# Two transformer layers in one kernel: layer 0's down projection as seven block products, with a new product order and modulation sums moved

## The chip, the cores and the metric

The kernel is one program on one core of a Trainium2 chip. The metric is device time in microseconds (us) for the whole program. All work is done by five engines with queues of their own: PE (TensorE, matrix products), DVE (VectorE), ACT (ScalarE), POOL (GpSimd) and SP (SyncE, which here issues most of the transfers). They meet through semaphores.

## The reference

Two layers on 1024 latent tokens of width 1024, beside 256 context tokens. Layer 0 mixes tokens with a gated MLP (gMLP), layer 1 with windowed attention; each is followed by a convolutional gated feed-forward network (ConvGLU). Cut to what matters here:

```python
def conv_ffn(h, w_up, conv_w, conv_b, w_down):
    a, b = jnp.split(h @ w_up, 2, axis=-1)
    ap = jnp.pad(a, ((0, 0), (1, 1), (0, 0)))
    a = ap[:, :-2] * conv_w[0] + ap[:, 1:-1] * conv_w[1] + ap[:, 2:] * conv_w[2] + conv_b
    return (jax.nn.gelu(a) * b) @ w_down
...
for i in range(DEPTH):
    mod_lat = (silu_c @ ada_w[i] + ada_b[i])[:, None, :]
    mod_ctx = (silu_cc @ ada_w[i] + ada_b[i])[None, None, :]
    sh1, sc1, g1, sh2, sc2, g2 = jnp.split(mod_lat, 6, axis=-1)
    ...
    x = x + g1 * rms_norm(y, norm_g[i, 1])
    h = modulate(rms_norm(x, norm_g[i, 2]), sh2, sc2)
    x = x + g2 * rms_norm(conv_ffn(h, ...), norm_g[i, 3])
```

The feed-forward width is 2816, or 22 blocks of 128. The same network also runs on the context tokens in layer 0; in layer 1 only the latent tokens are needed.

## The kernel before

Every fp32 product is made as three matmuls of 128x512 on parts of fewer bits: an operand x is split into xh (ACT's copy to a shorter format) and xl (DVE's x - xh), and hi*hi, hi*lo and lo*hi are summed in PSUM. So each weight or activation that comes in costs one ACT and one DVE operation before PE can use it. In names, wh/wl are the parts of weights, ah/al those of activations, "raw" (three buffers) is where most loads land, "row" a general tile of 128x1024 (ten buffers). PSUM is used as two psA tiles of two banks each and four psB tiles of one bank.

The stages on the time axis are: gMLP in two passes (`gmlp`: five token tiles, then five more, line 773), layer 0's feed-forward (`lat_ffn`, line 941, called on line 1651: its up stage on context, then on the latent tokens, then its down stage, then `ctx_down` for the context), attention, and layer 1's feed-forward (called on line 2058).

**Up stage.** For each block f of the 22 it makes seven products out of eight (sums of blocks of activations against sums of blocks of weights, a Winograd-Strassen scheme), then convolves, gates, and stores the result `actd[f]` in memory. ACT, DVE and POOL make the sums of weights, DVE the sums of results. The last f also runs `lead_in`, which loads the first operands of the down stage early.

**Layer 0's down stage** (in `lat_ffn`, `for h in range(2)`) is a plain loop: for each half h of the 1024 output columns, over 22 blocks n, over eight token tiles i, three matmuls into bank i: four banks of psA, four of psB. A half's banks are drained by `finish`, in the order of the tiles, then the other half begins on the same banks.

**Layer 1's down stage** (`down_blocks`, line 1338) uses seven products. The token tiles are split into two halves (i and i + 4), the columns into two of 512, and the 22 blocks into 11 pairs (f0, f1). Products p1 and p2 and p4 read activations as they are; p3, p5, p6 and p7 read the four sums of a pair. `pair_sums` makes those during the up stage: it loads both `actd` blocks, DVE adds four times, and stores the sums in `actc`. Eleven pairs are walked as six groups of two (the last has one). A product is 11 x 4 banks x 3 = 132 matmuls; p2 is added on top of p1 in the A banks (psA), the others use B banks (psB). `after(p)` drains banks to SBUF when a product ends: p1 by ACT's copies (s1), the others by DVE's adds into `ys`, which collects the result y. The weights' sums are made by DVE when a group is fetched (`fetch`, three groups ahead). The order was: p1, p6, p2's first group, p7, p2's second, p4, p2's third, p5, p3, and p2's last three groups as the tail, bank by bank, so that each token tile can leave as soon as its bank is done.

**Modulation sums.** mod_lat and mod_ctx are vectors of 6 x 1024 per layer, each piece called (l, m). A piece is summed by DVE over eight loads of 512 KB of `ada_w` (one operation of 128x1024 per load and per stream: latent, context), then turned into columns by PE's transposes (`ada_cols`). `ada_steps(l, m, streams)` is such a generator, and `step(gen)` runs it one step on at chosen points of a stage. Layer 0's pieces 0 to 4 are made in the gMLP passes. Layer 1's pieces 0, 1 (both streams), 3 and 4 (latent) are summed during layer 0's down stage (`sums_of`) and transposed during `ctx_down`.

The order in which each engine finally works is set by a scheduler from this program order and the buffers; the waits come from tiles: an operation that writes a PSUM tile waits for earlier readers of that tile, also when they read another bank of it.

Of the kernel before, what the change touches and what calls it, by code (L numbers as in the profile page):

```python
# [15 lines left out]
P = 128  # L16
D = 1024
# [15 lines left out]
def hybrid_kernel(  # L33
# [739 lines left out]
    def gmlp(si, hb, tiles, gate, extra, between, pre_last, on_flip=None, head=None, order=(0, 1, 2, 3, 4), mod=None):  # L773
# [5 lines left out]
        for nb in range(4):  # L779
# [3 lines left out]
            for u in range(4 if nb or not head else 0):  # L783
# [13 lines left out]
                if nb > 0:  # L797
                    step(extra)
# [142 lines left out]
    def lat_ffn(l, stage, n0, halos, gate, between, steady, ctx=None, after=None):  # L941
# [98 lines left out]
        def pair_sums(n, f0, f1):  # L1040
# [9 lines left out]
            V.tensor_tensor(out=s2, in0=s1, in1=a11, op=ALU.subtract)  # L1050
            Q.dma_start(actc[0:2, n].rearrange("s p c -> p s c"), u.rearrange("p (s c) -> p s c", s=2))
            yield
            V.tensor_tensor(out=s3, in0=a11, in1=a21, op=ALU.subtract)
            yield
            V.tensor_tensor(out=s4, in0=a12, in1=s2, op=ALU.subtract)
            Q.dma_start(actc[2:4, n].rearrange("s p c -> p s c"), w.rearrange("p (s c) -> p s c", s=2))
# [176 lines left out]
        for (f, how), nxt in zip(jobs, jobs[1:] + [None]):  # L1233
# [6 lines left out]
            if ctx is None:  # L1240
                fill_up[0] = sums_
# [7 lines left out]
        if ctx is None:  # L1249
# [3 lines left out]
        open_pool("down%d" % l)  # L1253
        pool = stage_pool["pool"]
        ks = list(range(n0, NF)) + list(range(n0))
        ys, sums = {}, []
        KEEP = 5
        if ctx is not None:
            extra = chain(*[sums_of(pool, sums, 1, m, streams)
                            for m, streams in ((0, (0, 1)), (1, (0, 1)), (3, (0,)), (4, (0,)))])  # L1260
        else:
            extra = iter(())

        def act_hl(k, own):
            raw = t_raw()
            Q.dma_start(raw, actd[k, :, 0:SEQ])
            hl = [t_w("w" + z) if own else pool.tile([P, 1024], F32R, name=nm("a" + z), tag="a" + z, bufs=7 if ctx is None else 6)
                  for z in "hl"]
            split_into(hl, raw)
            return hl  # L1270

        def finish(t, h, p, part):
            hs = slice(h * 512, (h + 1) * 512)
            junk = pool.tile([P, 512], mybir.dt.bfloat16, name=nm("junk"), tag="junk", bufs=2)
            if h == 0:
                ys[t] = pool.tile([P, 1024], F32, name=nm("y"), tag="y%d" % t, bufs=1)
            return gated(p, gate(t)[:, hs], ys[t][:, hs], part, junk)

        parts, hls = {}, {}
        for h in range(2):  # L1280
            pair = [psA() for _ in range(2)]
            banks = [pair[i // 2][:, i % 2, :] for i in range(4)] + [psB() for _ in range(4)]
            ws = {}

            def step_(n, i):
                (ah, al), (wh, wl) = hls[ks[n]], ws[n]
                tk = slice(i * P, (i + 1) * P)
                mm3(banks[i], ah[:, tk], al[:, tk], wh, wl, n == 0, n == NF - 1)

            def fetch(n):  # L1290
                if h == 0 or n >= KEEP:
                    hls[ks[n]] = act_hl(ks[n], h == 0 and n < 2)
                if n % 2 == 0:
                    raw = t_raw()
                    for j in range(2):
                        Q.dma_start(raw[:, j * 512:(j + 1) * 512],
                                    w_down[l][ks[n + j] * P:(ks[n + j] + 1) * P, h * 512:(h + 1) * 512])
                    hi, lo = t_w("wh"), t_w("wl")
                    split_into((hi, lo), raw)
                    for j in range(2):  # L1300
                        ws[n + j] = hi[:, j * 512:(j + 1) * 512], lo[:, j * 512:(j + 1) * 512]

            nk = NF - (2, 6 if ctx is None else 5)[h]
            if h == 1:
                ks.reverse()
            for n in range(nk):
                fetch(n)
                for i in range(8):
                    step_(n, i)
                if h or n < 14:  # L1310
                    step(extra, 1 + (n % 4 == 1))
            for n in range(nk, NF):
                fetch(n)
            for i in range(8):
                for n in range(nk, NF):
# [786 lines left out]
```

## Time and profile before

| what | value |
|---|---|
| time, median of 3 runs | 2903.92 us (2899.92 to 2905.09) |
| the profiled execution | 2896.91 us |
| its span | 2895.1 us |
| mean granted PE clock | 0.988 |
| PE busy | 2765.4 us, 14702 instructions |
| DVE busy | 2112.9 us, 3175 instructions |
| ACT busy | 1371.5 us |
| POOL busy | 676.2 us |
| DMA | 513.78 MB, mean 177 GB/s |

Times of windows and timelines are us from the start of the span. All operations go through one wrapper, so every row of the profile carries the same line (L50), and tiles tell them apart: `psA<-wh,ah` is a matmul of weights' high part and activations' high part into a psA tile. Stages begin at about: gMLP 66 and 400, layer 0's up stage 771 (context) and 917 (latent), its down stage 1343 and 1585 (context), attention 1655, layer 1's up stage 2240, its down stage 2670.

### The profile page before, as it was taken

What the parts mean: (1) busy time and instruction counts of PE and PEld (TensorE: products, weight loads), DVE (VectorE), ACT (ScalarE), POOL (GpSimd) and SP (SyncE); (2) the same over time, 40 slices, a digit from 0 to 9 for tenths busy, and PEclk for the clock granted to TensorE, in tenths of its full rate; (3) what the DMA queues carried; (4) which work ended last, traced back from release to release, by engine and by line L of the source; (5) the groups of instructions that cost most, each with busy time, mean ns of one, the idle gap of its engine ahead of it and who ended that gap; (6) DMA issues with size and microseconds to landing.
All of it is one profiled execution on the core that took longest, in us unless ns stands there. A gap on an engine that the chain in (4) does not pass through costs nothing. (4 is left out here: it accounts for less than half of the span.)

```text
span 2895.1 us, 40248 instructions
## 1 busy us (share of the span) xinstructions
PE 2765.4 (96%) x14702; PEld 2379.7 (82%) x14702; DVE 2112.9 (73%) x3175; ACT 1371.5 (47%) x2298; POOL 676.2 (23%) x1002
## 2 busy tenths in 40 slices
PE   7999999999999999999999999899996999999999
PEld 5798988899898888888877777788885988888787
DVE  6557675755887888778743669887876688888766
ACT  4332342322575444544323534777875444445333
POOL 1150130620201122220003024565552112111001
PEclk9999999999999999999999999999998999999999
DMA  8764357522585333546855865346576345445754
GB/s 260 242 192 151 112 175 220 169 89 83 187 236 178 111 100 117 167 160 210 299 167 174 281 209 193 114 156 234 173 238 200 107 152 188 150 152 178 244 180 149
DMA packets 418200, 513.78 MB, mean 177 GB/s; under 512 B 18641, under 2 KB 298065, under 8 KB 418001
## 3 DMA queue, kind: packets, MB, share of 16 engines
q1 hardware_dynamic: 361585, 448.01, 48.3%
q10 hardware_dynamic: 55264, 58.99, 6.0%
q0 software_dynamic: 1152, 4.19, 0.4%
q8 instruction: 116, 1.90, 0.3%
q14 instruction: 83, 0.68, 0.1%
HBM read 403.12 MB, written 108.00 MB: 177 GB/s over the span
## 5 line engine op out<-in xcount | busy, mean ns | idle before, releaser
L50 PE MATMUL psB<-cmb,wh 128*128 128x512 f32 (+2 forms) x2584 | 748.4, 374 | 5.8 <-ACT row L50 2.3
L50 ACT CAST wh<-raw 128x1024 fp32r<-128x1024 f32 (+1 forms) x378 | 334.1, 897 | 484.2 <-PE psB L50 178.6
L50 PEld LDWEIGHTS psB<-cmb,wh 128*128 128x128 f32 x2584 | 471.5, 188 | 95.5 <-ACT row L50 3.4
L50 PE MATMUL psB<-cmb,wl 128*128 128x512 f32 (+2 forms) x1292 | 482.6, 374 | 0.0
L50 DVE TENSOR_TENSOR wl<-raw,wh 128x1024 fp32r<-128x1024 f32 (+1 forms) x378 | 386.1, 1033 | 110.8 <-ACT wh L50 109.4
L50 PE MATMUL psB<-wh,big 128*128 128x512 f32 x864 | 286.3, 399 | 2.6 <-ACT big L50 1.3
L50 PEld LDWEIGHTS psB<-cmb,wl 128*128 128x128 f32 x1292 | 243.1, 188 | 43.5
L50 POOL TENSOR_SCALAR sm<-sm 128x1 f32<-128x1 f32 (+1 forms) x76 | 43.4, 572 | 925.9 <-ACT junk L50 371.8
L50 POOL TENSOR_TENSOR row<-raw,raw 128x512 f32<-128x512 f32 x44 | 73.7, 1675 | 594.2 <-DMA raw<-in_f_w_up_dram 477.1
L50 ACT CAST wh<-row 128x512 fp32r<-128x512 f32 (+1 forms) x152 | 120.2, 793 | 183.7 <-DVE row L50 95.0
L50 PE MATMUL psB<-wh,act 128*128 128x512 f32 x640 | 199.9, 390 | 1.6 <-DVE tmp L50 1.6
L50 PEld LDWEIGHTS psB<-wh,big 128*128 128x128 f32 x864 | 164.0, 191 | 39.5 <-ACT big L50 2.4
L50 PE MATMUL psA<-big,wh 128*128 128x320 f32 x1024 | 193.4, 311 | 2.8 <-ACT wh L50 1.7
L50 DVE SCALAR_TENSOR_TENSOR row<-row,cwcols,row 128x1024 f32<-128x1024 f32 (+2 forms) x142 | 153.2, 1079 | 36.6 <-ACT row L50 20.6
L50 ACT CAST ah<-raw 128x1024 fp32r<-128x1024 f32 (+1 forms) x77 | 77.5, 1010 | 192.3 <-PE psB L50 111.9
L50 PE MATMUL psB<-wl,big 128*128 128x512 f32 x432 | 167.0, 396 | 0.0
L50 PEld LDWEIGHTS psA<-big,wh 128*128 128x128 f32 x1024 | 159.8, 188 | 3.8 <-ACT wh L50 2.2
L50 DVE TENSOR_TENSOR al<-raw,ah 128x1024 fp32r<-128x1024 f32 (+1 forms) x77 | 90.2, 1174 | 94.0 <-ACT ah L50 93.9
L50 PE MATMUL psB<-wh,ah 128*128 128x512 f32 x388 | 152.0, 393 | 3.9 <-ACT wh L50 3.9
L50 POOL TENSOR_SCALAR row<-row,sm,sm 128x128 f32<-128x128 f32 x160 | 121.0, 771 | 147.6 <-DMA row<-vscr 133.3
L50 PE MATMUL psB<-wl,ah 128*128 128x512 f32 x388 | 152.2, 392 | 0.0
L50 PE MATMUL psB<-wh,al 128*128 128x512 f32 x388 | 152.0, 392 | 0.0
(277 smaller groups left out, 6193.6 us busy)
## 6 DMA issues: line engine op xcount, KB each, us to landing
raw<-in_f_w_up_dram SPq DMA_DIRECT2D x142, 512.0 KB, 4.6
raw<-in_a_w_in_dram SPq DMA_DIRECT2D x64, 512.0 KB, 4.7
raw<-in_ada_w_dram SPq DMA_DIRECT2D x64, 512.0 KB, 4.8
wh<-woscr SPq DMA_DIRECT2D x48, 512.0 KB, 4.8
raw<-actd SPq DMA_DIRECT2D x44, 512.0 KB, 4.7
actd<-row SPq DMA_DIRECT2D x39, 512.0 KB, 2.6
raw<-in_a_w_out_dram SPq DMA_DIRECT2D x35, 512.0 KB, 3.5
xT<-row ACTq DMA_DIRECT2D x33, 512.0 KB, 5.0
```

The costliest lines, as they stand in the source:

```text
L50: ins = fn(*a, **kw)
```

## The change

1. Layer 0's down projection now goes through `down_blocks` too, with a flag `inner`; the plain loop is gone. Layer 0's up stage therefore runs `pair_sums` and `lead_in`. `pair_sums` works in place, on two row tiles instead of four.
2. The products come in the order p1, p2, p6, p7, p4, p5, p3, in both layers; the last three groups of p3 are the tail. p5 and p3 have their banks C in psA. Each bank is drained right after its own last matmul. Loads of the weights that several products share come later.
3. A finished token tile goes to `leave`, which in layer 0 starts `lat_tail` (norm, store, flip into the next stage); the flips of tiles 4 to 7 wait for `held`.
4. Layer 1's modulation pieces 3 and 4 go to gMLP pass 0, pieces 0 and 1 (both streams) to pass 1, with more frequent steps.

The diff, cut to its core:

```diff
-                if nb > 0:
-                    step(extra)
+                if nb > 0 or not head:
+                    step(extra, 1 + (u % 2 if head else 0))
...
-            step(extra, 2 - f % 2)
+            step(extra, 2 if head else 2 - f % 2)
+        step(extra, 99)
...
-            u, w = t_row(), t_row()
-            s1, s2, s3, s4 = u[:, 0:512], u[:, 512:1024], w[:, 0:512], w[:, 512:1024]
-            V.tensor_tensor(out=s1, in0=a21, in1=a22, op=ALU.add)
...
+            V.tensor_tensor(out=a22, in0=a21, in1=a22, op=ALU.add)
+            yield
+            V.tensor_tensor(out=a21, in0=a11, in1=a21, op=ALU.subtract)
+            yield
+            V.tensor_tensor(out=a11, in0=a22, in1=a11, op=ALU.subtract)
+            Q.dma_start(actc[0:2, n].rearrange("s p c -> p s c"), r0.rearrange("p (s c) -> p s c", s=2))
+            yield
+            V.tensor_tensor(out=a12, in0=a12, in1=a11, op=ALU.subtract)
+            Q.dma_start(actc[2:4, n].rearrange("s p c -> p s c"), r1.rearrange("p (s c) -> p s c", s=2))
...
-                return W, lead_in() if ctx is None else iter(())
+                return W, lead_in()
...
-            if ctx is None and n >= 2 and n % 2 == 0:
+            if n >= 2 and n % 2 == 0:
                 step(sums_, 9)
                 sums_ = pair_sums(n // 2 - 1, *pairs[n // 2 - 1])
...
-        if ctx is None:
-            step(sums_, 9)
-            down_blocks(l, stage, gate, pairs, pair_sums(len(pairs) - 1, *pairs[-1]), early)
-            return
...
+        step(sums_, 9)
+        down_blocks(l, stage, gate, pairs, pair_sums(len(pairs) - 1, *pairs[-1]), early, ctx is not None)
         if ctx is not None:
-            step(extra, 99)
-            ctx_down(l, stage, gate, chain(*[ada_cols(1, m, st, accs, True) for m, st, accs in sums]), after)
+            ctx_down(l, stage, gate, after)
...
-        kinds = {"p5": 0, "p6": 1, "p7": 2, "p3": 3}
+        kinds = {"p6": 0, "p7": 1, "p3": 2, "p5": 3}
...
-        fillers = {"p6": 0, "p7": 1, "p4": 2}
-        for p in ("p1", "p6", "p7", "p4", "p5", "p3"):
-            seq += [(p, g) for g in range(NG)]
-            if p in fillers:
-                seq.append(("p2", fillers[p]))
-        tail = [("p2", g) for g in range(3, NG)]
...
+        order = ("p1", "p2", "p6", "p7", "p4", "p5", "p3")
+        seq = [(p, g) for p in order for g in range(NG)]
+        TAIL = 3
...
+                elif p == "p5":
+                    pc = [psA() for _ in range(2)]
+                    C = [pc[i // 2][:, i % 2, :] for i in range(4)]
+            banks = A if p in ("p1", "p2") else B if p in ("p6", "p7", "p4") else C
...
+                    mms(banks[i], p, g, [j], i, fresh and j == 0, last)
+                    if last:
+                        after(p, i)
...
+            for p, g in seq[-TAIL:]:
+                mms(C[i], p, g, list(range(len(members[g]))), i, False, g == NG - 1)
+            after("p3", i)
+            ss = gated(ys[i][:, 512:1024], gate(i)[:, 512:1024], ys[i][:, 512:1024], parts[i], junk(512))
+            leave(i, ss)
...
-    gmlp(1, hold["h"], MIX, gate_of(0, 2), chain(ada_steps(0, 3, (0, 1)), ada_steps(0, 4, (0, 1))),
+    gmlp(1, hold["h"], MIX, gate_of(0, 2), chain(ada_steps(0, 3, (0, 1)), ada_steps(0, 4, (0, 1)), ada_steps(1, 0, (0, 1)), ada_steps(1, 1, (0, 1))),
```

What this moves on the engines, in the compiled order, at three places.

PE in layer 1's down stage, where p1 ends, before. psA_24938 is p1's second two-bank tile; psB_25191 to 25194 are p6's banks:

```order
12617 L50 MATMUL psA_24938<-wh_25075,ah_25071 128x512
12618 L50 MATMUL psA_24938<-wl_25076,ah_25071 128x512
12619 L50 MATMUL psA_24938<-wh_25075,al_25072 128x512
12620 L50 MATMUL psB_25191<-wh_25116,ah_25112 128x512 [waits PE_49,Activation_49]
12621 L50 MATMUL psB_25192<-wh_25116,ah_25112 128x512 [waits PE_49]
```

The same place now. psA_25079 and psA_25080 are p1's and p2's two tiles; wh_25245 is p2's first weight:

```order
12488 L50 MATMUL psA_25079<-wh_25204,ah_25200 128x512 [waits Activation_49]
12489 L50 MATMUL psA_25079<-wl_25205,ah_25200 128x512
12490 L50 MATMUL psA_25079<-wh_25204,al_25201 128x512
12491 L50 MATMUL psA_25080<-wh_25204,ah_25200 128x512 [waits Activation_49]
12492 L50 MATMUL psA_25080<-wl_25205,ah_25200 128x512
12493 L50 MATMUL psA_25080<-wh_25204,al_25201 128x512
12494 L50 MATMUL psA_25079<-wh_25245,ah_25241 128x512 [waits Activation_49]
```

Before, p6 went on in other tiles. Now p1's last matmuls into the second bank of each tile wait for ACT, which drains the first, and p2's first one waits for ACT again. The same pattern stands where p5 ends and p3 begins, with DVE as the engine that drains.

SP's queue at the start of layer 1's down stage, before. row_24980 and 24981 hold the last pair's sums, raw_25103 is p6's first operand:

```order
906 L50 DMA raw_25064<-actd 128x512 [waits DMAHW1_49,Activation_49]
907 L50 DMA actc<-row_24980 128x2x512 [waits DMAHW2_49,DVE_49]
908 L50 DMA actc<-row_24981 128x2x512 [waits DMAHW3_49,DVE_49]
909 L50 DMA r_4267_24912<-in_f_w_down_dram 128x512 [waits DMAHW4_49]
910 L50 DMA r_4271_24916<-in_f_w_down_dram 128x512 [waits DMAHW5_49]
911 L50 DMA r_4271_24916<-in_f_w_down_dram 128x512 [waits DMAHW6_49]
912 L50 DMA r_4287_24932<-in_f_w_down_dram 128x512 [waits DMAHW7_49]
913 L50 DMA r_4287_24932<-in_f_w_down_dram 128x512 [waits DMAHW0_49]
914 L50 DMA raw_25103<-actc 128x2x512 [waits DMAHW1_49,Activation_49]
```

And now, where raw_25235 and row_25238 are p2's first activations and weights, raw_25275 its second activations, and row_25190 and 25191 the last pair's sums:

```order
979 L50 DMA raw_25235<-actd 128x512 [waits DMAHW2_49,Activation_49]
980 L50 DMA raw_25235<-actd 128x512
981 L50 DMA row_25238<-in_f_w_down_dram 128x512 [waits DMAHW4_49]
982 L50 DMA row_25238<-in_f_w_down_dram 128x512 [waits DMAHW5_49]
983 L50 DMA actc<-row_25190 128x2x512 [waits DMAHW6_49,DVE_49]
984 L50 DMA actc<-row_25191 128x2x512 [waits DMAHW7_49,DVE_49]
985 L50 DMA raw_25275<-actd 128x512 [waits DMAHW0_49,Activation_49]
```

The second product's first loads stand ahead of the stores of the last sums, and they read `actd`, not `actc`.

DVE in one f of layer 0's up stage, before. row<-psB are the sums of results, cwcols the convolution, gate the modulation sums for the gate:

```order
939 L50 TENSOR_TENSOR row_9252<-row_9252,s_9270 128x2x256
940 L50 TENSOR_TENSOR row_9252<-psB_9217,row_9252 128x2x256
941 L50 TENSOR_TENSOR wl_9329<-raw_9218,wh_9328 128x512
942 L50 TENSOR_TENSOR wl_9329<-raw_9219,wh_9328 128x512
943 L50 TENSOR_TENSOR row_9306<-psB_9216,s_9238 128x2x256
```

And now, in every second f:

```order
996 L50 TENSOR_TENSOR row_9313<-row_9313,s_9331 128x2x256
997 L50 TENSOR_TENSOR row_9355<-row_9354,row_9355 128x512
998 L50 TENSOR_TENSOR row_9354<-row_9354 128x512
999 L50 TENSOR_TENSOR row_9354<-row_9355,row_9354 128x512
1000 L50 TENSOR_TENSOR row_9355<-row_9355,row_9354 128x512
1001 L50 TENSOR_TENSOR row_9313<-psB_9278,row_9313 128x2x256
1002 L50 TENSOR_TENSOR wl_9395<-raw_9279,wh_9394 128x512
```

The four adds of a pair (row_9354 and row_9355) stand together, ahead of the operation that reads the next bank of results.

More of the change, by code (lines that the diff above doesn't have):

```diff
@@ L1264, in act_hl @@
[L1264 to L1315, printed above, removed]
-                    step_(n, i)
-                if h == 0:
-                    parts[i] = finish(i, 0, banks[i], EPS)
-                    continue
-                ss = finish(i, 1, banks[i], parts[i])
-                if ctx is not None:
-                    active.append(lat_tail(stage, i, ys[i], ss))
-                    tick()
-                    continue
-                xr = t_row()
-                Q.dma_start(xr[:, 0:1024], src_row(stage, i))
-                r = t_sm(1)
-                G.tensor_tensor(out=r, in0=ss, in1=mhalf, op=ALU.pow)
-                for q in range(2):
-                    hs = slice(q * 512, (q + 1) * 512)
-                    V.scalar_tensor_tensor(out=xr[:, hs], in0=ys[i][:, hs], scalar=r, in1=xr[:, hs],
-                                           op0=ALU.mult, op1=ALU.add)
-                    Q.dma_start(out[0, i * P:(i + 1) * P, hs], xr[:, hs])
@@ L1334, in lat_ffn, with down_blocks @@
-        if ctx is not None:
-            step(extra, 99)
-            ctx_down(l, stage, gate, chain(*[ada_cols(1, m, st, accs, True) for m, st, accs in sums]), after)
-    def down_blocks(l, stage, gate, pairs, rest, early):
+        step(sums_, 9)
+        down_blocks(l, stage, gate, pairs, pair_sums(len(pairs) - 1, *pairs[-1]), early, ctx is not None)
+        if ctx is not None:
+            ctx_down(l, stage, gate, after)
+    def down_blocks(l, stage, gate, pairs, rest, early, inner):
         open_pool("down%d" % l)
@@ L1385, in fetch @@
             for second, m in side_loads.get((p, g), ()):
+                if second and m not in r22:
+                    r22[m] = t_row()
                 w_part((r12, r22)[second][m], m, second, 1)
@@ new lines, in lower @@
+        def lower(t):
+            ss = t_sm(1)
+            S.activation(junk(1024), ys[t], AF.Square, accum_out=ss)
+            G.tensor_scalar(out=ss, in0=ss, scalar1=1.0 / D, scalar2=EPS, op0=ALU.mult, op1=ALU.add)
+            V.tensor_tensor(out=ys[t], in0=ys[t], in1=gate(t), op=ALU.mult)
+            leave(t, ss)
+        parts, held, chores = {}, [True], []
+        order = ("p1", "p2", "p6", "p7", "p4", "p5", "p3")
+        seq = [(p, g) for p in order for g in range(NG)]
+        TAIL = 3
@@ L1525, in down_blocks @@
             while chores:
-                chores.pop(0)()
-            for p, g in tail:
-                mms(A[i], p, g, list(range(len(members[g]))), i, False, g == NG - 1)
-            final(i, A[i])
-    def sums_of(pool, sums, l, m, streams):
-        accs = [pool.tile([P, 1024], F32, name=nm("dacc"), tag="dacc%d%d" % (m, s), bufs=1) for s in streams]
-        yield from ada_sums(l, m, streams, accs,
-                            lambda: pool.tile([P, 1024], F32, name=nm("araw"), tag="araw", bufs=2))
-        sums.append((m, streams, accs))
@@ L1537, in lat_tail @@
-    def lat_tail(stage, t, y, ss):
+                lower(chores.pop(0))
+            for p, g in seq[-TAIL:]:
[3 more added lines that the diff above has]
+            leave(i, ss)
+            if inner:
+                tick()
+    def lat_tail(stage, t, y, ss, held, wide):
         xr = t_row()
@@ L1545, in lat_tail, with ctx_down @@
         S.dma_start(xs[stage + 1][t * P:(t + 1) * P, :], xr)
-        for _ in range(4):
+        while held[0]:
             yield 0
-        flip(stage + 1, t, y, True)
-    def ctx_down(l, stage, gate, cols, after):
+        for _ in range(4 if wide else 1):
+            yield 0
+        flip(stage + 1, t, y, wide)
+    def ctx_down(l, stage, gate, after):
         banks = [[psB() for h in range(2)] for i in range(2)]
@@ L1592, in ctx_down @@
                 pass
-            step(cols, 99)
             build_h = after()
```

134 lines of the change are left out of this document (46 added, 88 removed).

## The prediction

> **What bounds the kernel now.** I read the page first, for the shares of the engines; then the chain of waits, for what TensorE waits on; then the windows by stage, for what each stage leaves idle; and last the timelines where the chain or the windows showed a hole. The page:
>
> ```profile
> span 2895.1 us, 40248 instructions
> PE 2765.4 (96%) x14702; PEld 2379.7 (82%) x14702; DVE 2112.9 (73%) x3175; ACT 1371.5 (47%) x2298; POOL 676.2 (23%) x1002
> ```
>
> TensorE is busy 96% of the span, VectorE 73%. The time is the number of matmuls and the few holes between them. By stage (the columns are start:end, length, busy time and count of PE, PEld, DVE, ACT, POOL, then granted clock, DMA share, GB/s):
>
> ```profile
> 66.00:400.00 334.00, 328.99 (x1826) 292.59 (x1825) 219.69 (x334) 115.09 (x159) 71.58 (x102) 1.00 0.55 172
> 400.00:770.00 370.00, 366.59 (x2004) 325.26 (x2004) 227.82 (x319) 125.28 (x176) 101.57 (x119) 1.00 0.47 148
> 917.00:1338.00 421.00, 419.74 (x1851) 347.49 (x1852) 336.98 (x385) 203.85 (x299) 83.39 (x94) 1.00 0.39 128
> 1343.00:1585.00 242.00, 237.30 (x1050) 195.51 (x1048) 140.57 (x127) 77.24 (x104) 20.96 (x35) 0.99 0.66 225
> 1585.00:1655.00 70.00, 63.16 (x311) 50.70 (x309) 48.74 (x64) 38.36 (x50) 12.05 (x16) 0.98 0.88 285
> 2330.00:2670.00 340.00, 336.01 (x1660) 283.15 (x1659) 283.43 (x361) 163.86 (x256) 65.63 (x78) 1.00 0.50 164
> 2670.00:2890.00 220.00, 214.92 (x932) 176.03 (x930) 158.85 (x164) 89.78 (x111) 12.34 (x19) 0.98 0.59 193
> ```
>
> The rows are the two gMLP passes, layer 0's up stage on the latent tokens, its down stage, the context's down stage, layer 1's up stage (most of it) and layer 1's down stage. In the up stages and gMLP passes TensorE idles for 1.3 to 5.0 us of hundreds, so work added to other engines there costs nothing until it breaks through. The down stages hold the holes.
>
> **The change, part by part.** *Matmuls.* Layer 1's down stage already works by block products, and the chain of waits prices them:
>
> ```profile
> 2744.69 29.92 PE psB L50 x132
> ...
> 2815.41 59.91 PE psB L50 x264
> ```
>
> 132 matmuls, one block product, take 29.92 us (0.2267 us each); two in a row take 59.91, so a boundary between products on single-bank tiles costs nothing. Layer 0's down projection goes from 22 x 8 x 2 x 3 = 1056 matmuls to 7 x 132 = 924. It is one block product less, on the engine that sets the time: **-29.9 us**.
>
> *The hole between layer 0's two halves.* The old loop does columns 0 to 511 for all eight token tiles, then the other half, on the same eight banks. The timeline of PE at that place:
>
> ```profile
> 1448.24 0.39 PE L50 MATMUL psB<-wl,ah 128*128 128x512 f32 x1
> 1453.23 0.79 PE L50 MATMUL psA<-wh,ah 128*128 128x512 f32 x1 [4.61 <-DVE y L50]
> 1453.82 0.63 PE L50 MATMUL psA<-wl,ah 128*128 128x512 f32 x1
> 1454.25 0.63 PE L50 MATMUL psA<-wh,al 128*128 128x512 f32 x1
> 1454.68 0.63 PE L50 MATMUL psA<-wh,ah 128*128 128x512 f32 x1
> ...
> 1456.50 0.40 PE L50 MATMUL psB<-wl,ah 128*128 128x512 f32 x1
> ```
>
> From 1448.24 to 1456.50 stand nine starts; at 0.2267 they would take 2.04 us, and they took 8.26. 4.6 of the lost 6.2 us is the wait for VectorE to drain a bank, the rest the wider spacing (0.43) of the matmuls behind it. The loop goes, and the hole with it: **-6.2 us**.
>
> *The hole in layer 1 behind the first product.* There p6 came second and needs the pair sums of the last pair, which go from VectorE to memory and back. PE's timeline:
>
> ```profile
> 2705.85 2.07 PE L50 MATMUL psB<-wh,ah 128*128 128x512 f32 x4 [3.93 <-ACT wh L50]
> ```
>
> In two stretches of equal length, one with the hole and one without:
>
> ```profile
> 2700.00:2750.00 50.00, 46.04 (x190) 37.06 (x189) 41.39 (x40) 22.56 (x26) 0.00 (x0) 0.93 0.60 205
> 2750.00:2800.00 50.00, 50.00 (x222) 41.42 (x221) 34.56 (x34) 17.05 (x18) 0.00 (x0) 1.00 0.53 168
> ```
>
> 32 matmuls fewer at 0.2267 are 7.2 us. In the new order p2 follows p1. It reads the activations as they are, no sums, and its first loads stand ahead of the last pair's stores in SyncE's queue; p6 comes 30 us later. **-7.2 us**.
>
> *New waits in the new order.* The first and last products of the old code ended in banks that the next product left alone. Now p2 goes on in p1's banks, and p5 and p3 share one pair of two-bank tiles. In the program's order the last matmuls into the second bank of a tile wait for the drain of the first, and the next product's first ones for the drain of the second. The drains cost (groups of layer 1's down stage, and VectorE where p5 ends):
>
> ```profile
> L50 ACT COPY s<-psA 128x512 f32<-128x512 f32 x4 | 2.2, 586 | 2.9 <-PE psA L50 2.9
> 2843.33 0.69 DVE L50 TENSOR_TENSOR y<-psB,y 128x512 f32<-128x512 f32 x1 [2.90 <-PE psB L50]
> 2843.94 1.22 DVE L50 TENSOR_TENSOR al<-raw,ah 128x1024 fp32r<-128x1024 f32 x1
> 2845.07 1.88 DVE L50 TENSOR_TENSOR y<-psB,y 128x512 f32<-128x512 f32 x3
> ```
>
> One drain by ScalarE is 0.59, one by VectorE 0.69. Three matmuls into another tile (0.68 us) lie between, so a pair of tiles hides about one drain of two. I estimate 0.8 us for p1 to p2 and 1.7 for p5 to p3, where VectorE has its split of operands (1.2 us) queued in between; twice 2.5 is **+5.0 us**. The ends are 0 (all four hidden) and 2 x 4 x (0.6 + 0.7) = 10.4 (every drain shown), before any loss of clock.
>
> Does a hole of about a microsecond also slow the matmuls behind it? In the first gMLP pass:
>
> ```profile
> 270.51 0.50 PE L50 MATMUL psB<-wl,act 128*128 128x512 f32 x1 [1.00 <-DVE wl L50]
> 270.85 0.63 PE L50 MATMUL psB<-wh,act 128*128 128x512 f32 x2
> ```
>
> The three starts behind this 1.00 us hole are at most 0.34 us apart, so hardly anything is added; behind the hole of 4.61 us they stood at 0.43. I add no clock loss. [...]
>
> *The tail.* The last 60 matmuls are p3's, not p2's; behind the last one VectorE now adds before the gate is applied: one 0.69 us drain, **+0.7 us**.
>
> *Pair sums in layer 0's up stage* (per pair: two loads and two stores of 512 KB, four adds of 128x512). Price of an add and the state of VectorE in one f of 19.04 us:
>
> ```profile
> L50 DVE TENSOR_TENSOR row<-row,s 128x512 f32<-128x512 f32 x44 | 29.9, 679 | 0.0
> 1023.63 1.27 DVE L50 SCALAR_TENSOR_TENSOR gate<-raw,ccols,gate 128x1024 f32<-128x1024 f32 x1
> ...
> 1027.41 0.69 DVE L50 TENSOR_TENSOR row<-psB,row 128x512 f32<-128x512 f32 x1 [0.77 <-PE psB L50]
> ...
> 1030.13 0.69 DVE L50 TENSOR_TENSOR row<-psB,s 128x512 f32<-128x512 f32 x1 [0.82 <-PE psB L50]
> ...
> 1032.24 3.52 DVE L50 SCALAR_TENSOR_TENSOR row<-row,cwcols,row 128x1024 f32<-128x1024 f32 x2 [0.82 <-issue]
> 1035.68 2.32 DVE L50 SCALAR_TENSOR_TENSOR gate<-raw,ccols,gate 128x1024 f32<-128x1024 f32 x1
> ```
>
> Four adds are 2.7 us per pair, two f apart; VectorE idles 0.77 + 0.82 + 0.82 = 2.4 us in each f, 4.8 per pair, so they fit. Forty-four adds put its load at (337.0 + 29.9) / 421 = 87%. Layer 1's up stage already carries the same sums at 283 of 340 us (83%): TensorE idles 3.99 us there (1.2%) against 1.26 (0.3%) in layer 0's, a difference of 3.7 us over 421. That is the near end; the far ones are 0 and all ten early pairs in full, 27 us. I take **+2.0 us**, nearer layer 1's row since other things make holes there too.
>
> [...]
>
> *Layer 2's modulation sums* (32 loads of 512 KB, 48 VectorE operations, 48 transposes, 12 reductions) move from the two down stages into the gMLP passes, 16 operations into the first, 32 into the second. On TensorE they move at the same count. Price in the gMLP passes:
>
> ```profile
> L50 DVE SCALAR_TENSOR_TENSOR acc<-raw,ccols,acc 128x1024 f32<-128x1024 f32 x56 | 70.9, 1290 | 70.8 <-DMA raw<-in_ada_w_dram 70.8
> ```
>
> Each takes 1.29 us and held VectorE another 1.26 until its load was there; behind it queue the splits of the next weights, on which TensorE waits. VectorE gets 16 x 2.55 = 41 us on 220 of 334, and 32 x 2.55 = 82 on 228 of 370: 78% and 84%. The two passes idle 5.0 + 3.4 = 8.4 us with 56 such operations; 48 more in proportion are 7.2, if none of it shows 0. I take **+2.0**, since VectorE's waits are mostly covered by weights that are ready early.
>
> *Start of the context's down stage.* Its row idles 70.0 - 63.2 = 6.8 us. The transposes and their waits leave it, which may give back up to half; new is that four tiles' flips into the next stage now crowd there on ScalarE. Ends -3 and +5, I take **+1.6**. What DMA the down stage loses (0.66 of its engines) isn't on TensorE's path.
>
> Sum: -29.9 - 6.2 - 7.2 + 5.0 + 0.7 + 2.0 + 2.0 + 1.6 = **-32.0 us**. The profiled execution took 2896.9 us (1.8 beyond its span); that makes 2864.9. The median shown, 2903.9, lies 7.0 above the profiled one: **2872**.
>
> **The rivals.**
> *A, the boundaries are dearer* (chance 0.16). Every new hole grows past what 270.51 bore, and the clock drops. The hole of 4.61 us lost 1.6 us beyond its idle time, the one of 3.93 lost 3.3. Four times some 2 us more is +8: 2880. Against it: the drains are under a microsecond.
> *B, the holes come back elsewhere* (0.15). p2 now needs, per group of 24 matmuls (5.44 us), 512 KB of activations, 512 KB of weights and about 512 KB for later products: 1.57 MB, 289 GB/s. The context's down stage ran at 285 with 0.88 of the DMA engines busy and idled. If p2 is held by its loads in both layers, about 6 us each, the two holes are only moved: -32 + 12 = -20, 2884.
> *C, slower* (0.03). [...]
> *D, the change doesn't do what it says* (0.01): the compiled order has 132 matmuls of that form fewer, so the first term stands.
> Forecast: 0.65.
>
> **Numbers.** The low end is the forecast with the soft costs (11.3) near zero, 2862; the high end takes in A and B (2884) and 4 us for the spread of runs, 2888. About 0.2%, 5.8 us, is what a measurement of this kernel can tell from no change. Forecast, A and B all lie beyond it: faster 0.95; between, C at half its price: 0.03; slower 0.02.
>
> **What would show it.** Right: layer 0's down stage runs 924 matmuls as seven stretches near 29.9 us; no 4.6 us hole in it; behind layer 1's p1 no wait for reloaded sums; holes under 1 us at p1 to p2 and p5 to p3, spacing unchanged behind them; up stage of layer 0 within 2 us of 421. Wrong: PE idle of over 1 us per pair in that stage, clock under 0.98 in the down stages, gMLP passes longer than by the moved transposes, or p2 waiting for loads.

## The result, and the profile after

The changed kernel takes 2888.68 us (median of 6 runs, 2880.38 to 2894.62) against 2904.45 us before (6 runs, 2899.92 to 2908.94): ratio 0.9944, 95% interval 0.9926 to 0.9962. It is faster by 16 us, half of the 32 forecast, and lies just above the range's upper end of 2888. The profiled executions differ by 11.9 us of span, less than the medians' 15.8: both profiled runs are shorter than their medians, before's by 7.5 us, after's by 3.7. The page of after:

```profile
span 2883.2 us, 40248 instructions
PE 2746.3 (95%) x14570; PEld 2358.2 (82%) x14570; DVE 2211.3 (77%) x3292; ACT 1386.1 (48%) x2317; POOL 707.4 (25%) x998
```

PE has 132 matmuls fewer, as forecast, but is busy for a smaller share: 19 us of work went, 12 us of time. To see where, I cut both executions at the same events. The rows are, in turn: gMLP pass 0, pass 1, the context's up stage, layer 0's latent up stage, its latent down stage (from the first to the last matmul on tiles named ah or al), the context's down stage, layer 1's down stage, and the tail behind PE's last matmul. Windows of before:

```profile
23.37:406.39 383.02, 375.46 (x2033) 329.25 (x2033) 258.64 (x395) 139.36 (x194) 77.11 (x108) 1.00 0.56 178
406.39:770.38 363.99, 360.58 (x1978) 320.31 (x1976) 223.33 (x315) 121.16 (x170) 96.04 (x114) 1.00 0.48 149
770.38:913.63 143.25, 131.19 (x1082) 127.73 (x1081) 114.71 (x172) 100.39 (x171) 11.49 (x54) 0.98 0.80 236
913.63:1336.27 422.64, 420.91 (x1858) 348.10 (x1857) 339.25 (x388) 204.59 (x300) 83.95 (x95) 1.00 0.39 127
1347.37:1584.33 236.96, 232.26 (x1024) 191.34 (x1023) 136.20 (x122) 74.40 (x100) 20.30 (x35) 0.99 0.66 224
1584.33:1666.94 82.61, 75.02 (x362) 60.13 (x361) 55.64 (x69) 44.65 (x57) 12.72 (x16) 0.98 0.85 276
2682.36:2888.95 206.59, 202.56 (x877) 165.82 (x875) 147.06 (x152) 82.00 (x102) 12.11 (x18) 0.98 0.57 187
2888.95:2895.10 6.15, 0.00 (x0) 0.00 (x0) 2.10 (x3) 0.69 (x2) 0.81 (x2) 0.84 0.45 168
```

And of after:

```profile
22.93:414.95 392.02, 379.36 (x2048) 332.76 (x2049) 279.81 (x420) 137.46 (x193) 97.59 (x108) 1.00 0.63 196
414.95:787.18 372.23, 365.37 (x2009) 323.05 (x2008) 266.70 (x359) 122.83 (x171) 102.92 (x114) 1.00 0.54 168
787.18:931.98 144.80, 133.43 (x1083) 130.63 (x1081) 114.23 (x172) 100.74 (x172) 9.97 (x54) 0.95 0.80 234
931.98:1357.03 425.05, 422.80 (x1858) 349.09 (x1856) 364.04 (x428) 204.67 (x300) 79.99 (x95) 1.00 0.53 176
1368.13:1578.18 210.05, 204.71 (x901) 167.57 (x899) 144.22 (x145) 89.83 (x118) 28.06 (x33) 0.99 0.59 197
1578.18:1661.03 82.85, 72.45 (x307) 55.24 (x305) 51.78 (x53) 45.96 (x60) 11.73 (x15) 0.94 0.80 264
2669.38:2872.93 203.55, 200.10 (x877) 163.76 (x875) 144.04 (x151) 80.09 (x101) 9.99 (x16) 1.00 0.57 187
2872.93:2883.20 10.27, 0.00 (x1) 0.00 (x0) 4.81 (x7) 0.77 (x3) 2.59 (x4) 0.67 0.30 111
```

The lengths, row by row, against the terms of the forecast:

| stretch | forecast, us | measured, us |
|---|---|---|
| both gMLP passes | +2.0 | +9.0 + 8.2 = +17.2 |
| layer 0's latent up stage | +2.0 | +2.4 |
| layer 0's down stage, latent and context | -29.9 - 6.2 + 2.5 + 1.6 = -32.0 | -26.9 + 0.2 = -26.7 |
| layer 1's down stage up to PE's end | -7.2 + 2.5 = -4.7 | -3.0 |
| tail | +0.7 | +4.1 |
| all else | 0 | -5.9 |
| sum | -32.0 | -11.9 |

The largest miss, 15 us, is in the gMLP passes, with 15 and 31 more PE instructions, 21 and 43 us more of VectorE, and 5 and 3 us more idle time of TensorE. "All else" is mostly attention up to layer 1's up stage, 535.2 before and 530.6 after. The three kernels with the old down stage of layer 0 take 535.2 to 536.1 us there, the ten with the new one and the same attention 526.7 to 534.8, so a part of it may be the change's; why wasn't tried.

### The profile page after: what moved, and what is told of

Read it like the earlier page. It is cut to its first block, busy times and chain, and to the rows that moved or that the text cites. A ratio compares the mean times of both kernels' runs of the same rounds, so it can differ in the third digit from the quotient of the medians.

```text
span 2883.2 us, 40248 instructions
## 1 busy us (share of the span) xinstructions
PE 2746.3 (95%) x14570; PEld 2358.2 (82%) x14570; DVE 2211.3 (77%) x3292; ACT 1386.1 (48%) x2317; POOL 707.4 (25%) x998
## 5 line engine op out<-in xcount | busy, mean ns | idle before, releaser
L50 ACT CAST wh<-raw 128x1024 fp32r<-128x1024 f32 (+1 forms) x344 | 299.0, 884 | 447.5 <-PE psB L50 158.2
L50 DVE TENSOR_TENSOR wl<-raw,wh 128x1024 fp32r<-128x1024 f32 (+1 forms) x344 | 346.2, 1019 | 82.5 <-ACT wh L50 81.3
L50 ACT CAST wh<-row 128x1024 fp32r<-128x1024 f32 (+1 forms) x196 | 162.5, 834 | 185.8 <-DVE row L50 90.9
L50 POOL TENSOR_TENSOR row<-raw,raw 128x512 f32<-128x512 f32 x44 | 67.9, 1543 | 594.5 <-DMA raw<-in_f_w_up_dram 453.4
L50 DVE SCALAR_TENSOR_TENSOR acc<-raw,ccols,acc 128x1024 f32<-128x1024 f32 x105 | 135.5, 1307 | 90.8 <-DMA raw<-in_ada_w_dram 90.7
L50 DVE TENSOR_TENSOR wl<-row,wh 128x1024 fp32r<-128x1024 f32 (+1 forms) x196 | 185.6, 950 | 13.8 <-ACT wh L50 13.8
L50 ACT CAST ah<-raw 128x1024 fp32r<-128x1024 f32 x80 | 77.5, 974 | 208.2 <-PE psB L50 83.9
L50 POOL TENSOR_SCALAR row<-row,sm,sm 128x128 f32<-128x128 f32 x160 | 142.5, 909 | 116.3 <-DMA row<-vscr 100.4
L50 DVE TENSOR_TENSOR row<-row,row 128x512 f32<-128x512 f32 (+3 forms) x167 | 152.7, 917 | 19.4 <-DMA row<-actd 9.6
L50 DVE TENSOR_TENSOR al<-raw,ah 128x1024 fp32r<-128x1024 f32 x80 | 90.2, 1128 | 77.0 <-ACT ah L50 76.6
```

Source lines behind the costliest of these rows:

```text
L50: ins = fn(*a, **kw)
```

## The experiments

Each run is timed beside the kernel before on its chip; a ratio is to that, with its 95% interval. Stage lengths are from the same events as above; the first expectations give lengths between other events (357 and 374 us for the passes, 229 and 223.4 for the down stages), of which only the differences compare. Each length is of one execution. How far they vary by themselves is seen from the kernels that do the same work in a stretch (their number in brackets):

| stretch, us | old code there | new code there |
|---|---|---|
| both gMLP passes | 746.8 and 747.0 (2) | 762.1 to 767.9 (7) |
| layer 0's latent up stage | 422.1 to 423.2 (3) | 420.6 to 425.1 (11) |
| layer 0's latent down stage | 237.0 and 238.3 (2) | 208.9 to 211.2 (10) |
| the context's down stage | 82.6 and 83.2 (2) | 80.8 to 83.7 (9) |
| layer 1's down stage up to PE's end | 205.8 and 206.6 (2) | 201.5 to 204.6 (10) |
| tail | 6.2 (2) | 10.3 to 10.9 (10) |

So the passes cost 15 to 21 us, not exactly 17.2, and a difference of 1 to 3 us in a stage is not shown by its length alone.

**What the moved sums cost, and what moving them gave back.** The first kernel leaves them out:

```diff
-         chain(ada_steps(0, 0, (1,)), ada_steps(0, 1, (1,)), ada_steps(0, 2, (0, 1)), ada_steps(1, 3, (0,)),
-               ada_steps(1, 4, (0,))),
+         chain(ada_steps(0, 0, (1,)), ada_steps(0, 1, (1,)), ada_steps(0, 2, (0, 1))),
...
-ada_steps(0, 4, (0, 1)), ada_steps(1, 0, (0, 1)), ada_steps(1, 1, (0, 1))),
+ada_steps(0, 4, (0, 1))),
```

> The changed kernel without layer 1's modulation pieces 0, 1, 3 and 4: their loads, sums, transposes and reductions are left out of the gMLP passes, and their columns are set to one. It prices what the moved sums cost where they now stand. Theory 1 (TensorE is the bound in the gMLP passes, so 48 transposes of 0.23 to 0.27 us and the waits behind VectorE are paid in full): pass 0 falls from 357 to about 348 us, pass 1 from 374 to about 364, the whole by 16 to 19 us. Theory 2 (the prediction's price: the sums are hidden and cost 2, the other 16 us came from elsewhere): the passes stay within 4 us of 357 and 374 and the whole falls by 2 to 4.

Measured: 2868.39 us, ratio 0.9889 (0.9872 to 0.9906); the whole falls by some 16 us by the ratios. The passes:

```profile
23.53:407.72 384.19, 375.87 (x2033) 330.67 (x2033) 259.74 (x397) 138.80 (x194) 94.71 (x108) 1.00 0.57 179
407.72:773.40 365.68, 361.30 (x1977) 319.78 (x1976) 224.35 (x313) 121.40 (x170) 84.34 (x114) 1.00 0.46 147
```

Of the 17.2 us, 14.4 go with the sums. Theory 1 stands, a little under its numbers (7.8 and 6.5 us, not 9 and 10); theory 2 falls. The other 2.9 us remain without them, which is within what the passes vary by.

The second kernel is the one before with the move alone:

```diff
-            extra = chain(*[sums_of(pool, sums, 1, m, streams)
-                            for m, streams in ((0, (0, 1)), (1, (0, 1)), (3, (0,)), (4, (0,)))])
+            extra = iter(())
```

(and the gMLP lines of the change).

> The kernel before with one part of the change alone: layer 1's modulation pieces go to the gMLP passes, everything else as before. Theory 1 (the context's down stage has TensorE waiting for transfers, so 48 transposes cost little there, and cost full price in the gMLP passes): gMLP passes up by 16 to 19 us, layer 0's down stage unchanged at 229, the context's down stage shorter by 3 or less; the whole is slower than before by 13 to 18 us. Theory 1b (the transposes and their waits were paid in the context's down stage too): that stage falls by 8 to 12 us, the whole is slower by 5 to 10. Theory 2 (the prediction): plus 2, less up to 3, no measurable difference.

Measured: 2902.19 us, ratio 1.0005 (0.9995 to 1.0014): no difference, the sum of theory 2, but not by its way. The gMLP passes are up by 21 us in its profiled execution, which is the longest of its ten (2909.66, the others 2898.39 to 2903.08); its span is 13 us longer than that of before's profiled run, where the medians differ by 1, so the 21 is more than a typical run would show, by how much no trace tells. Against that, layer 0's down stage, the plain loop with all its 1056 matmuls, shrank:

```profile
1369.85:1600.72 230.87, 230.79 (x1025) 190.44 (x1023) 83.20 (x76) 74.08 (x100) 20.27 (x35) 1.00 0.47 157
1600.72:1680.93 80.21, 71.85 (x314) 56.34 (x313) 48.41 (x48) 44.32 (x56) 12.03 (x16) 0.96 0.86 284
```

It takes 6.1 us less and has no hole at all, with the two halves on the same banks as ever; in the run of the order alone (below), which keeps loop and sums, the hole of 4.61 us is there again. VectorE's timeline of before at the hole shows why:

```profile
1445.03 1.29 DVE L50 SCALAR_TENSOR_TENSOR dacc<-araw,ccols,dacc 128x1024 f32<-128x1024 f32 x1 [2.20 <-DMA araw<-in_ada_w_dram]
1450.69 0.75 DVE L50 TENSOR_SCALAR dacc<-araw,ccols 128x1024 f32<-128x1024 f32 x1 [4.38 <-DMA araw<-in_ada_w_dram]
1451.36 1.22 DVE L50 TENSOR_TENSOR wl<-raw,wh 128x1024 fp32r<-128x1024 f32 x1
1452.49 0.68 DVE L50 TENSOR_TENSOR y<-psA,gate 128x512 f32<-128x512 f32 x1
```

The drain of the bank (y<-psA) stood behind a modulation sum that waited 4.38 us for its load. So the hole came from the sums in that queue, and the loop without them has none. Theory 1 missed here: it had that stage unchanged and the whole 13 to 18 us slower. The 48 transposes that left the context's stage shortened it by 2.4 us, no more than its length varies by itself.

Two more kernels split the price: one without the transposes and reductions, one without 28 of the 32 loads.

```diff
         yield from ada_sums(l, m, streams, accs)
+        if l == 1 and m in (0, 1, 3, 4):
+            for q in range(len(streams)):
+                G.memset(mod_cols(l, m, q), 1.0)
+            return
```

> The changed kernel with the loads and sums of the four moved pieces kept in the gMLP passes, but their 48 transposes and 12 reductions left out (their columns are set to one). With all of it left out, the two passes took 384.2 and 365.7 us against 392.0 and 372.2. Theory 1 (the price is TensorE's own work: 16 and 32 transposes, each 0.11 to 0.27 us): the passes fall to about 388 and 366, pass 1 almost all the way. Theory 2 (the price is VectorE's queue and the landing buffers, that is the sums and loads): the passes stay above 390 and 370.

```diff
-            raw = (space or t_raw)()
-            Q.dma_start(raw, ada_w[l, k * P:(k + 1) * P, m * D:(m + 1) * D])
+            own = l == 1 and m in (0, 1, 3, 4) and k > 0
+            if not own:
+                raw = (space or t_raw)()
+                Q.dma_start(raw, ada_w[l, k * P:(k + 1) * P, m * D:(m + 1) * D])
...
+ in0=acc if own else raw
```

> The changed kernel with 28 of the 32 moved loads left out (the sums then add a tile to itself, so VectorE's operations, the transposes and the reductions all stay). Theory 1 (TensorE's own work is the price): no change, 392 and 372 us. Theory 2 (VectorE waits in its queue for these loads, 1.26 us each before the change, and the splits of weights wait behind it): pass 0 falls by 4 us or more, to 388 or less, and the idle time of TensorE in it from 13.6 to under 10.

Without transposes: ratio 0.9913 (0.9898 to 0.9928), passes 387.2 and 368.9. Without loads: 0.9933 (0.9913 to 0.9952), passes 390.8 and 370.4.

```profile
23.79:411.02 387.23, 376.71 (x2032) 330.92 (x2033) 278.55 (x413) 138.79 (x194) 96.08 (x108) 1.00 0.63 199
411.02:779.89 368.87, 361.85 (x1978) 319.66 (x1976) 260.48 (x345) 121.67 (x170) 106.33 (x114) 1.00 0.53 168
```

The rows are those without transposes. The transposes and their reductions, which are VectorE's, make 4.8 + 3.4 = 8.2 of the 17.2 us, 6.2 of it busy time of TensorE; the sums with their loads make 756.1 - 749.9 = 6.2, and 2.9 is left. The first is clear of the spread, and by the ratios the whole fell by 9 us; the second is barely clear of it, and that the 2.9 is the new stepping isn't shown. The loads alone gave 3.0, which the spread covers, and theory 2 fails on both of its numbers: pass 0 takes 390.8 us, not 388 or less, and TensorE idles 12.1 us in it, not under 10. Theory 1 alone isn't the whole either, since the passes without transposes stay 9 us above before's. By these numbers the transposes with their reductions are the largest part, just under half.

**Can the sums stand better?** Slower stepping in pass 0, and pieces 3 and 4 in attention:

```diff
-                    step(extra, 1 + (u % 2 if head else 0))
+                    step(extra)
```

> The changed kernel with the modulation sums of gMLP pass 0 stepped once per unit in its first part, as before the change; the same sums, only later. In the run without the moved sums a hole of 4.1 us at 96 us stayed, where before's is 0.45. Theory 1 (the hole is the faster stepping: VectorE's sums stand in its queue ahead of a copy of psA on which PE waits): the hole falls to about 0.5 us and pass 0 from 392 to about 388 measured from the first big matmul to the last one on activations, the whole by 4. Rival (the hole comes with the pass's other differences): 4 us or more stay.

```diff
+    later = chain(ada_steps(1, 3, (0,)), ada_steps(1, 4, (0,)))
...
+        if 1 <= i < 20:
+            step(later)
```

> The changed kernel with layer 1's pieces 3 and 4 summed and transposed in the first part of the attention loop instead of gMLP pass 0, whose stepping is as before the change. Theory 1 (a sum costs what TensorE can't hide: full price in the gMLP, less where TensorE idles, as it does for 53 of 611 us in attention): pass 0 returns to about 383 us (from 392), attention grows by 0 to 5 us, the whole falls by 4 to 9. Rival (attention is held by VectorE, 489 of 611 us busy, in a chain with ScalarE): attention grows by 15 us or more and the whole is slower.

The old rate: ratio 0.9939 (0.9920 to 0.9958), pass 0 391.95 us. The hole at 96 us is gone, as theory 1 said, but two others came, 3.33 us before a matmul on wl and 2.86 before transposes of acc, and the pass is as long: the expected 4 us didn't come. In attention: ratio 0.9973 (0.9963 to 0.9983), 2891.49 us, slower than after. Pass 0 returned to 381.7, but attention grew by 15.3 over after, beyond its spread:

```profile
1650.46:2196.33 545.87, 499.63 (x3052) 434.14 (x3053) 457.08 (x1073) 354.84 (x812) 275.17 (x429) 0.98 0.62 204
```

The rival's sizes came: idle time of TensorE in this stage was not room for more work on VectorE, which is now busy for 457 of its 546 us. That VectorE is what holds attention was not tried apart.

**Layer 0's end.** After shows two holes where PE stands before flips (the transposes that carry a finished token tile into the next stage):

```profile
1569.00 1.89 PE L50 MATMUL psB<-ident,y 128*128 128x128 f32 x8 [3.28 <-POOL y L50]
1570.54 0.77 PE L50 MATMUL psA<-wh,ah 128*128 128x512 f32 x1
1571.11 0.63 PE L50 MATMUL psA<-wl,ah 128*128 128x512 f32 x1
1571.54 0.63 PE L50 MATMUL psA<-wh,al 128*128 128x512 f32 x1
...
1585.09 1.97 PE L50 MATMUL psA<-ident,y 128*128 128x128 f32 x8 [4.78 <-POOL y L50]
```

```diff
-        for _ in range(4 if wide else 1):
+        for _ in range(6 if wide else t + 1):
             yield 0
-        flip(stage + 1, t, y, wide)
+        flip(stage + 1, t, y, True)
```

> The changed kernel with the flips of layer 0's finished token tiles put later in the program, behind the first products of the context's down stage and all in psA tiles, instead of between the last matmuls of the latent down stage. Theory 1 (PE stands 3.3 and 4.8 us in front of flips whose tile norm POOL has not finished, and runs slower for some microseconds after each): both holes go, the stretch from the first matmul of the down stage to the start of attention falls by 8 to 13 us from 293. Rival (the context's down stage is held by its transfers, 0.83 of the DMA engines busy, and the next stage waits for the flips anyway): the holes go but the stretch falls by under 3 us, with the waits moved to the weights of the context's products or to attention's start.

Measured: ratio 0.9949 (0.9929 to 0.9969), as after.

```profile
1367.28:1570.15 202.87, 200.56 (x877) 163.55 (x875) 144.98 (x146) 86.38 (x112) 24.31 (x26) 1.00 0.58 196
1570.15:1662.20 92.05, 74.95 (x330) 59.35 (x329) 50.26 (x52) 47.79 (x68) 16.95 (x22) 0.91 0.77 252
```

The down stage falls by 7.2 us, the context's grows by 9.2: both holes are gone, and others stand in their place. The largest, with ScalarE in front of it:

```profile
1579.34 1.22 PE L50 MATMUL psB<-wh,wh 128*128 128x512 f32 x2 [6.85 <-ACT wh L50]
1577.20 1.06 ACT L50 ACTIVATE y<-row 128x1024 bf16<-128x1024 f32 x1 [4.74 <-DVE row L50]
1578.26 1.03 ACT L50 CAST wh<-raw 128x1024 fp32r<-128x1024 f32 x1
```

The rival's sizes came, but this hole isn't a wait for a transfer: the split of the context's weights (wh) stands in ScalarE's queue behind an operation of a token tile's tail, which waited 4.74 us for VectorE, and starts as soon as that is done. So this run shows that the wait moved, not that transfers hold the stage. For that, half of its weights' loads are left out:

```diff
-            raw = t_raw()
-            Q.dma_start(raw, w_down[l][k * P:(k + 1) * P, :])
+            if k % 2 == 0:
+                raw = t_raw()
+                Q.dma_start(raw, w_down[l][k * P:(k + 1) * P, :])
```

> The changed kernel with every second load of weights in the context's down stage left out (the block loaded before is used twice; all splits and matmuls stay). Theory 1 (that stage is held by its transfers, which is why neither 48 transposes fewer nor the late flips shortened it): the stretch from the last latent matmul to attention falls from 82.9 to 75 or less. Rival (it is held by the tiles' norms and flips, or by splits): it stays above 80.

Measured: ratio 0.9910 (0.9893 to 0.9928), the stage 74.6 us, with both holes (3.27 and 4.78) still there:

```profile
1581.26:1655.85 74.59, 69.30 (x306) 56.63 (x305) 51.34 (x53) 45.39 (x61) 12.85 (x15) 0.93 0.68 225
```

That is clear of the 80.8 to 83.7 of the others, and no wait for a split of weights over 0.6 us is left in it. So transfers hold that stage for some 8 us, beside the flips. What TensorE was spared there, 48 transposes or the holes, came back little or not at all.

**Layer 1's down stage.** The new order alone, in the kernel before:

```diff
-        for p in ("p1", "p6", "p7", "p4", "p5", "p3"):
+        order = ("p1", "p2", "p6", "p7", "p4", "p5", "p3")
```

(with the rest of the new product code and the in-place sums, for layer 1 alone).

> The kernel before with another part alone: layer 1's down stage takes the new product order, the in-place pair sums and the new tail; layer 0 keeps its plain loop and the sums stay where they were. Theory 1 (the hole behind p1 shrinks from 3.9 to 2.5 us since the drains stand behind a split that waits for its load, and the tail grows by 4 since each add stands behind the previous tile's last operation): layer 1's down stage within 2 us of before's 223.4, PE's part of it 3 us shorter and the tail 4 us longer; the whole not measurably different. Theory 2 (the prediction): the stage falls by 4 us.

Measured: ratio 1.0002 (0.9992 to 1.0012). PE's part 202.41 (206.59 before), the tail 10.31 (6.15): 4.2 gained, 4.2 lost, near theory 1's 3 and 4; the hole behind p1 is 1.20 us here, not the 2.5 it named. PE and ScalarE in after, where p1 ends:

```profile
2686.83 0.39 PE L50 MATMUL psA<-wh,al 128*128 128x512 f32 x1
2689.69 0.50 PE L50 MATMUL psA<-wh,ah 128*128 128x512 f32 x1 [2.47 <-ACT s L50]
2690.02 0.40 PE L50 MATMUL psA<-wl,ah 128*128 128x512 f32 x1
2690.26 0.40 PE L50 MATMUL psA<-wh,al 128*128 128x512 f32 x1
```

```profile
2688.11 1.04 ACT L50 CAST ah<-raw 128x1024 fp32r<-128x1024 f32 x1 [5.79 <-DMA raw<-actd]
2689.06 1.07 ACT L50 COPY s<-psA 128x512 f32<-128x512 f32 x2
```

ScalarE idled 5.79 us in front of a split for p2's second group, with p1's drains (s<-psA) behind it. The mend:

```diff
-                split_into([t[:, 0:n] for t in hl], raw[:, 0:n])
...
+            late_split = p in ("p1", "p5") and g == NG - 1
+            while splits and not late_split:
+                splits.pop(0)()
...
+                        tc.keep_in_program_order(cast)
```

> The changed kernel with the split of p2's second group pinned behind the four drains of p1 on ScalarE, in both layers (the load itself stays early). Theory 1 (the 2.47 us hole behind layer 1's p1 is the drain standing behind a split that waits for its load): the hole falls to under 1 us, layer 1's down stage by 2 to 3 us, layer 0's by 0 to 1. Rival (p2's own operands are late and the drains only seem to be the cause): a hole of 2 us or more stays, put down to a load or a split. The whole moves by less than a measurement can tell.

Measured: ratio 0.9939 (0.9919 to 0.9958). The hole is one of 0.67 us. PE's part of the stage is 201.84 (203.55), a difference that its spread covers; layer 0's is 209.42 (210.05). ScalarE at that place:

```profile
2682.08 0.59 ACT L50 COPY s<-psA 128x512 f32<-128x512 f32 x1 [3.28 <-PE psA L50]
2683.72 1.07 ACT L50 COPY s<-psA 128x512 f32<-128x512 f32 x2 [1.06 <-PE psA L50]
2686.05 0.59 ACT L50 COPY s<-psA 128x512 f32<-128x512 f32 x1 [1.26 <-PE psA L50]
2686.54 1.05 ACT L50 CAST ah<-raw 128x1024 fp32r<-128x1024 f32 x1
```

The drains now wait for PE alone, and the split comes last. Theory 1 holds for the cause. The ten kernels that have the new order without this mend bear it out: the later the split starts, the longer the hole, one for one. Four of them, from the first matmul on ah of the stage:

| kernel | the split starts, us | hole of TensorE, us |
|---|---|---|
| without transposes | 16.49 | 0.23 |
| order alone | 17.46 | 1.20 |
| flips late | 18.32 | 2.07 |
| after | 18.73 | 2.47 |

In all ten the hole is the split's start less 16.26. So the 2.47 of after is the longest of them; on average it is 1.3, and the mend, with a steady 0.67, is worth some 0.7 us here, not the 2 to 3 expected.

The tail of after, in the chain of waits, one tile of four:

```profile
2871.56 0.61 DVE y L50
...
2872.25 0.73 ACT junk L50 x2
...
2873.08 0.76 POOL sm L50
...
2873.91 0.55 POOL sm L50
...
2874.49 1.41 DVE row L50 x2
2875.90 0.61 DVE y L50
```

A tile takes 4.3 us here (2871.56 to 2875.90), while PE makes a bank's last 15 matmuls in 3.4: the next drain (y) waits behind the last product (row) of this tile, which waits for POOL's root.

```diff
+            if done:
+                leave(*done.pop(), True)
+            done.append((i, ss))
...
+                if pin:
+                    tc.keep_in_program_order(stt)
```

> The changed kernel with layer 1's tail reordered on VectorE: the last two operations of a token tile are pinned behind the drain and the gate product of the next one. Theory 1 (the tail is 10.3 us behind PE's last matmul against 6.2 before because each drain stands behind the previous tile's last operation, which waits for POOL): the tail falls to 7 or less, the whole by 3 to 4. Rival (the tail is the longer chain of one tile, add, square, root, product, whatever the order): 9.5 to 10.3, no change.

Measured: ratio 0.9930 (0.9912 to 0.9948), an interval that overlaps after's; the tail 8.07 us, not the 7 that theory 1 asked for. Half of what was lost came back: theory 1 holds for 2.2 us of 4.1. What the rest is wasn't tried apart; the last tile's own chain is one more operation long.

Both mends together (the two diffs above):

> The changed kernel with the two mends that helped: the split behind p1's drains in both layers, and the tail's last operations pinned behind the next tile's drain. Expected from the single runs: layer 1's down stage 2 us shorter, the tail 2 us, the whole 4 to 5 us under the changed kernel, ratio to before about 0.993. Rival (effects of this size are lost in the spread of the executions): ratio 0.994 to 0.995.

Measured: 2880.23 us, ratio 0.9932 (0.9917 to 0.9946); the hole 0.68, the tail 8.69. Both mends show in the trace; PE's part, 202.18, lies within the spread of the kernels without them, and the interval overlaps that of after (0.9926 to 0.9962), so a gain of the whole of some 3.5 us is not shown.

## Where the prediction was right and where it failed, point by point

*132 matmuls, -29.9.* Right as counted. Layer 0's two down stages gave 26.7 together, and the hole's 6.2 is in it, so 9.4 us came back. Among them are the waits at the products' boundaries, 0.83 and 0.87 us (2.5 was forecast), and the two holes before flips, 3.28 and 4.78, which the kernel before doesn't have; the rest wasn't taken apart.

*The hole between the halves, -6.2.* The size was right, the reason wrong. The prediction read "the wait for VectorE to drain a bank" as the loop's fault; the trace had the sum ahead of the drain in VectorE's queue, one row up. The move of the sums alone removes it, so it paid for a part of the move; whether the block products alone would have removed it, no run shows.

*Layer 1's hole, -7.2, and the new waits, +2.5 a layer.* The stage gained 3.0, not 4.7, a difference that its spread nearly covers. No wait for reloaded sums is left behind p1, as forecast; the new wait was 2.47 us, not 0.8 (0.23 to 2.47 in the ten kernels), because I priced the drain by its own 0.59 us and not by what stands ahead of it in ScalarE's queue. At p5 to p3, 1.7 was forecast, and the hole is 0.87 in both layers. In rows 1450.69 (VectorE, before) and 2688.11 (ScalarE, after) a drain stood behind an operation that waited for a load, for 4.38 and 5.79 us.

*Tail, +0.7.* Mis-sized: +4.1. One more operation per tile was counted at the end of the chain once; it stands in each of the four tiles, behind the tile before. The pinned order shows this for 2.2 us; the rest stays open.

*Pair sums in layer 0's up stage, +2.0.* Measured +2.4, for 40 more operations of VectorE and 25 us of its time. But after is the longest of the eleven kernels with these sums (420.6 to 425.1 us); the three without take 422.1 to 423.2. So no cost of the sums is shown, and the agreement is luck. Rival C, slower, did not come, and no run shows the price that the chances count by half. What after's trace shows is the adds of this stage (three of a pair's four; the fourth is listed apart):

```profile
L50 DVE TENSOR_TENSOR row<-row,row 128x512 f32<-128x512 f32 x30 | 20.6, 687 | 1.7 <-DMA row<-actd 1.1
```

They took 0.69 us each, with 1.1 us of waiting for loads in the whole stage.

*Modulation sums (layer 1's, which the prediction calls layer 2's), +2.0.* This is the step that failed: 17.2 us measured. "On TensorE they move at the same count" took a moved transpose for free, though it left a stage that waits for transfers, where some 2.4 us were saved, and came into stages where TensorE was 98 and 99% busy before: 8.2 us with the reductions. For the rest I scaled the passes' idle time, 7.2 as the upper end, and then took 2.0 "since VectorE's waits are mostly covered"; measured 9.0, of it 6.2 with the sums and their loads and 2.9 without them. What the 6.2 is made of stays open: leaving out the loads didn't separate it.

*Context's stage, +1.6.* Measured +0.2, but not by the sum's way: the flips waited for POOL's norm, not for ScalarE, and their new wait of 4.78 us stands against 48 transposes and some waits that went. Transfers hold a part of that stage, which the sum didn't have.

Rival A's loss of clock did not come: the granted clock is 0.99 and 1.00 in the two layers' latent down stages, and behind the hole of 2.47 the matmuls stand 0.33 and 0.24 us apart. Rival B's price (2884) came near to the result by luck: p2's late load held TensorE through ScalarE's queue, for 2.47 us in layer 1 and 0.83 in layer 0, not for 6 in each, and the largest miss is in the gMLP passes.

## What to carry to other kernels

Before calling a moved operation neutral, ask what the old stage and the new one wait for: here work taken from a stage that is held by transfers saved little there (some 2.4 us), and cost more where the engine that does it bounds the new stage (8.2 us). Price a drain or any operation on which the bounding engine waits by what stands ahead of it in its queue, above all by a split or sum that waits for a load: the holes traced here (1450.69, 2688.11, the tail, and the late flips' 6.85) were a short operation behind a waiting one. And see whether the next thing in line is ready before mending a hole: the late flips took 7.2 us from one stage and put 9.2 into the next. A stage's length in one trace can't carry a gain of 1 to 3 us: look how it varies in kernels that left it alone, and read the rows.

## What the runs showed of the hardware

Behind the idle time of 2.47 us at 2689.69 TensorE's matmuls stood 0.33 and 0.24 us apart; behind the one of 3.28 at 1569.00 and the eight transposes that follow it, 0.57 and 0.43, against 0.227 in a full stretch. No single length divides the two cases in these traces: a hole of 2.40 us at 2003.97 in before is followed by starts 0.60 and then 0.43 apart, one of 2.75 at 1750.21 in the kernel without 28 of the loads by none above 0.34 until the next hole, 0.44 at 1753.29. What ran before each of them differs too, and no run separates that.

48 transposes of 128x128, listed at 0.27 us each, cost with their 12 reductions on VectorE 8.2 us in passes where TensorE is 97 and 98% busy, or 0.17 per transpose.
